# Four instead of three seven-product items in ten of twenty gate and up blocks, the norm's factor moved into the down product, and the mixer's constants moved to its own pool

## The chip, the cores and the metric

The kernel runs on one core of a Trainium2 chip, as one program. The metric is the time of one execution on the device in microseconds (us). The median of three runs of the kernel before is 2236.44 us (2235.84 to 2237.41). One more execution was profiled; its trace is what the figures of engines, lines and waits are read from.

TensorE (PE in the profile) multiplies; VectorE (DVE), ScalarE (ACT) and GpSimd (POOL) do element work; SyncE (SP) issues most transfers. Each engine works through its own list of instructions in order and waits on semaphores where an operand is not ready.

## What is computed

One decoder layer on `x` of 256 tokens by 2048 features, all float32:

```python
x = x + 0.5 * swiglu(rms_norm(x, ffn1_norm), ffn1_w_gate, ffn1_w_up, ffn1_w_down)
x = gated_parallel_mixer(x, ...)        # windowed attention beside an RWKV-7 recurrence
x = memory_cross_attention(x, mem, ...)
x = x + 0.5 * swiglu(rms_norm(x, ffn2_norm), ffn2_w_gate, ffn2_w_up, ffn2_w_down)
return rms_norm(x, final_norm)

def swiglu(h, w_gate, w_up, w_down):    # widths 2048 -> 5632 -> 2048
    return (jax.nn.silu(h @ w_gate) * (h @ w_up)) @ w_down
```

A norm's per-token factor `r` (called `rs` or `ms` in the trace) commutes with a product of matrices, so the kernel multiplies the un-normed `x` (with the gain on its features) by the weights and applies `r` to the result: `silu(r * gate)` and `r * up`.

## The kernel before

**Precision.** Each float32 weight tile is divided on chip into `hi` and `lo`, whose sum it is: ACT makes `hi` (L330), DVE makes `lo = raw - hi` (L331). `x` is divided likewise (`xhi`, `xlo`). One product of a 128x128 piece of `x` with a 128x512 piece of weights is three matmuls: hi by xhi, lo by xhi and hi by xlo (L422, L423, L424). Matmuls of the FFNs write 512 columns.

**Blocks and items.** Each of the two FFNs handles its 5632 columns in 11 blocks of 512, in groups of 4, 4 and 3 blocks, each group followed by its part of the down product. Block 0 is done with plain products; blocks 1 to 10 by `gate_up`, which calls `product_pair`. A block there is a row of eight items, q = 0 to 7. An item holds two of the 16 slices of 128 features (k-tiles) of the gate's and of the up's weights, four tiles of 128x512. A plain item takes eight products, 24 matmuls. An item of the other kind, a "seven", takes the seven products of a Strassen-like scheme on its 2x2 arrangement, 21 matmuls, on sums and differences of weight tiles and of pieces of `x`.

**What a seven needs.** `sums` forms the weights' differences on DVE: L350 (128x1024), L351 and L352 (128x512 each). ACT divides them into `thi` (L355, two of 128x1024), DVE into `tlo` (L356, two). There is one buffer of `thi` and one of `tlo`, so a seven's new `thi` can be written only when PE is done with that of the last seven. The tiles used as they are go through L330 and L331. The sums of `x` (`chi`, `clo`) are made once for each FFN by `combinations`, in the background of the first blocks; a chunk q whose item is a seven has four-term sums, and chunks 1 and 3, plain items between sevens, have a difference of two (`EARLY`). `SEVEN = (0, 2, 4)` says which items of a block are sevens; `SEVEN_DOWN = (2, 4)` does it for the down product's pairs.

**Order.** `next_item` hands out an item and divides the one ahead (`AHEAD`); `hi` and `lo` have three buffers, the weights' landing tiles (`raw2`) three. Background generators put work in between at each tick, and a scheduler orders the instructions of each engine by its own estimate of their times. The order is thus fixed when the kernel is built.

**End of a block.** `gate_up` adds the banks of PSUM: L559 to L561 after the last seven; at the block's end L567 and L570 on the gate's two halves, with SiLU on ACT behind each (L568, L571, `r` as its scale), and for the up's two halves L574 (add) and L575 (`scalar_tensor_tensor`, times `r` and times the gate), 128x512 each. In `down`, the factor 0.5 of the residual is applied in each `scalar_tensor_tensor` of `half` and, for pairs that are not done as sevens, at L778.

**Norms and constants.** `rs` of a norm is made from DVE's `ms` (L716) by POOL (L718). The masks and small matrices that the mixer needs (`identr`, `abias`, `mask3`, `bdmean`, `center`, `keep` and others, L213 to L244) are made by POOL at the kernel's start, in a pool that lives to its end, ahead of POOL's transfers of `attn_sinks`, `g_later` and `v_rwkv` (L247, L252). Copies of `x` to DRAM (`x1d`, L840) go out from POOL ahead of the mixer.

Of the kernel before, what the change touches and what calls it, by code (L numbers as in the profile page):

```python
# [15 lines left out]
P = 128  # L16
# [24 lines left out]
EARLY = tuple(q for q in range(max(SEVEN)) if q not in SEVEN)  # L41

SEVEN_DOWN = (2, 4)
# [46 lines left out]
def feed_forward_plan(wg, wu, wd):  # L90
    for gi, (j0, nj) in enumerate(GROUPS):
        for j in range(j0, j0 + nj):
            if j == 0:
                for w in (wg, wu):
                    yield w, 0, KD, j * 512, 512
            else:
                yield (wg, wu), 0, KD, (j * 512, j * 512), SEVEN
# [43 lines left out]
def decoder_layer(ctx: ExitStack, tc: tile.TileContext, a: dict, out: bass.AP):  # L141
# [71 lines left out]
    identr = cpool.tile([P, P], F32R, name="identr")  # L213
    select(identr[:], ones[:], [[-1, P]], ALU.is_equal, 0.0, 0, 1)
    abias = cpool.tile([P, 2, P], F32R, name="abias")
    pool.memset(f32(abias[:]), 0.0)
    select(abias[:, 0, :], abias[:, 0, :], [[1, P]], ALU.is_gt, NEG, 0, -1)
    select(abias[:, 1, :], abias[:, 1, :], [[-1, P]], ALU.is_ge, NEG, 0, 1)

    ups = cpool.tile([P, P], F32, name="ups")  # L220
    pool.memset(ups[:], UP)
    mask3 = cpool.tile([P, 3, P], F32, name="mask3")
    select(mask3[:, 0, :], ups[:], [[1, P]], ALU.is_gt, 0.0, 0, -1)
    select(mask3[:, 1, :], ups[:], [[1, P]], ALU.is_ge, 0.0, 0, -1)
    select(mask3[:, 2, :], ups[:], [[1, P]], ALU.is_ge, 0.0, 0, -1)

    mask_l = cpool.tile([P, P], F32, name="mask_l")
    select(mask_l[:], ups[:], [[-1, P]], ALU.is_gt, 0.0, 0, 1)
    bdones = cpool.tile([P, P], F32, name="bdones")
    bdmean = cpool.tile([P, P], F32, name="bdmean")  # L230
    bdup = cpool.tile([P, P], F32, name="bdup")
    pool.memset(bdones[:], 0.0)
    pool.memset(bdmean[:], 0.0)
    pool.memset(bdup[:], 0.0)
    for e in range(2):
        q = slice(64 * e, 64 * e + 64)
        pool.memset(bdones[q, q], 1.0)
        pool.memset(bdmean[q, q], 1.0 / 64)
        pool.memset(bdup[q, q], UP)
    center = cpool.tile([P, P], F32, name="center")  # L240
    dve.tensor_tensor(center[:], ident[:], bdmean[:], ALU.subtract)
    keep = cpool.tile([P, 2, P], F32, name="keep")
    pool.memset(keep[:], 1.0)
    pool.memset(keep[:, :, 0:1], 0.0)  # L244
# [23 lines left out]

    gneps = cpool.tile([P, 1], F32, name="gneps")
# [164 lines left out]
    def combinations(sp, x, seven, early, ready, tag, apart):  # L434


        n = 4 * len(seven) + 2 * len(early)
        parts = [sp.tile([P, n, P], F32R, tag=tag + e, name=tag + e) for e in ("hi", "lo")]
        c = {"parts": parts, "at": {}, "next": []}

        def work():
# [4 lines left out]
            for q in sorted(seven + early):  # L446
                while not all(KU * q + i in x.done for i in range(KU)):
                    yield
                v = sp.tile([P, 2, 2, P], F32, tag="u", name="u", bufs=2)
                f = sp.tile([P, 4, P], F32, tag="u", name="u", bufs=2)  # L450
                n = 4 if q in seven else 2
                s = slice(o, o + n)
                with behind_weights():
                    dve.tensor_tensor(
                        v[:].rearrange("p k t n -> p k (t n)"), f32(x.at(0, 2 * q, 2)),
                        f32(x.at(1, 2 * q, 2)), ALU.add,
                    )
                    if q in seven:
                        dve.tensor_tensor(f[:, 0], v[:, 0, 1], v[:, 1, 1], ALU.add)
                        dve.tensor_tensor(f[:, 1], f[:, 0], v[:, 0, 0], ALU.subtract)  # L460
                        dve.tensor_tensor(f[:, 2], v[:, 0, 0], v[:, 0, 1], ALU.subtract)
                        dve.tensor_tensor(f[:, 3], v[:, 1, 0], f[:, 1], ALU.subtract)
                    else:
                        dve.tensor_tensor(f[:, :2], v[:, :, 0], v[:, :, 1], ALU.subtract)
                yield from idle(2)
                with behind_weights():
                    act.copy(parts[0][:, s], f[:, :n])
                yield from idle(2)
                with behind_weights():
                    dve.tensor_tensor(  # L470
                        parts[1][:, s], f[:, :n], f32(parts[0][:, s]), ALU.subtract
                    )
                c["at"][q] = o
                o += n
                yield
# [4 lines left out]
    def product_pair(x: Act, c, w, four, seven, early, after, end, finish, first=()):  # L480
# [10 lines left out]
        def bank(to):  # L491
            if to in b:
                return
            for pair in PAIRS:
                if to in pair:
                    banks = two()
                    b.update((e, banks[:, i]) for i, e in enumerate(pair))
                    return
# [13 lines left out]
        def of_c(q, i):  # L512
            return [p[:, c["at"][q] + i, :] for p in c["parts"]]

        p5 = "p8" if four else "p5"
        for q in range(late + 1):
# [3 lines left out]
            if q in seven:  # L520
# [16 lines left out]
                continue  # L537
            u = next_item()
            for i in range(KU):
                for to, t, j in (("p2", 0, 0), ("p4", 1, 0), ("p3", 0, 1), (p5, 1, 1)):  # L540
                    off = to == "p3" and q in early
                    ends = last and i == KU - 1
                    add(to, of_c(q, i) if off else of_x(t, k + i), u[i][j], ends)
# [1193 lines left out]
```

## Time and profile before

| what | before |
| --- | --- |
| median of three runs | 2236.44 us (2235.84 to 2237.41) |
| the profiled execution, its time | 2236.75 us |
| its span in the trace | 2235.0 us |
| PE busy (matmuls) | 2216.0 us, 99% |
| DVE busy | 1745.4 us, 78% |
| ACT busy | 1193.5 us, 53% |
| POOL busy | 81.3 us, 4% |
| granted TensorE clock | 0.999 |

The span is the time between the first and the last instruction of the trace; the execution's time is 1.75 us longer, and that is 0.31 us above the median of the runs. A row of a timeline gives the start, the duration, the engine, the line of the code, the operation with its output and inputs, their shapes, and in brackets how long the engine was idle before it and what released it. Instructions of one engine overlap: the next one can begin before the last has ended, so the distance between two starts is what a row of instructions costs, not the sum of durations. Lines of the kernel before are L330 and so on; the same statements stand 15 to 25 lines further down in the changed one (L350 there is L365, L356 is L371, L331 is L346).

### The profile page before, as it was taken

To read this page: it belongs to the slowest core of one execution; us is meant where nothing else is said; L and a number is where in the kernel's file an instruction comes from. 1 tells how busy PE (TensorE), PEld (TensorE's weight loads), DVE (VectorE), ACT (ScalarE), POOL (GpSimd) and SP (SyncE) were. 2 spreads that over 40 slices of the span, in tenths; PEclk is the share of its full clock that TensorE was granted. 3 is DMA by queue.
4 is the path that set the end of the run, shared out by engine and by line. 5 is a ranking of instruction groups with operands and counts; after the bars stand their busy time and mean duration, and the time that the engine had idled before them with its cause. 6 is when DMAs were issued, how large, how long until landed. Compare 5 with 4: busy or idle time off the path is not lost.

```text
span 2235.0 us, 28341 instructions
## 1 busy us (share of the span) xinstructions
PE 2216.0 (99%) x10792; PEld 1819.2 (81%) x10792; DVE 1745.4 (78%) x2039; ACT 1193.5 (53%) x1434; POOL 81.3 (4%) x151
## 2 busy tenths in 40 slices
PE   9999999999999999999999999999999999999998
PEld 7888888888888877788888878888888888888886
DVE  7988988898987567886465466558888888898887
ACT  6555555555555567444443445556555555555554
POOL 1000000000000000103200100001000000000000
PEclk9999999999999999999999999999999999999999
DMA  7666665566556545677435775547665656566664
GB/s 247 211 220 195 203 207 190 187 208 202 194 193 214 165 130 151 219 219 233 121 102 148 230 266 189 181 164 255 201 207 177 218 193 199 193 202 194 207 203 155
DMA packets 219832, 435.40 MB, mean 195 GB/s; under 512 B 13888, under 2 KB 16016, under 8 KB 219696
## 3 DMA queue, kind: packets, MB, share of 16 engines
q1 hardware_dynamic: 210768, 406.37, 56.8%
q0 software_dynamic: 8352, 26.44, 3.8%
q8 instruction: 84, 1.38, 0.3%
q10 hardware_dynamic: 576, 0.79, 0.1%
q14 instruction: 52, 0.43, 0.1%
HBM read 420.05 MB, written 13.50 MB: 194 GB/s over the span
## 4 chain that ended last, share of the span: by engine, by line
PE 93%; DVE 3%; DMA 2%; ACT 1%; issue 1%; SPq 0%; POOLq 0%; POOL 0%; DVEq 0%; ACTq 0%
PE acc L422 20%; PE acc L423 20%; PE acc L424 20%; PE two L422 9%; PE two L423 9%; PE two L424 9%; PE two L185 2%; DVE lo L331 1%; PE two L177 1%; DMA raw<-in_ffn_w_up_dram 1%; DMA raw<-in_w_proj_rwkv_dram 1%; ACT hi L330 0%; PE two L1279 0%; DMA raw<-in_ffn_w_gate_dram 0%; PE acc L1416 0%
## 5 line engine op out<-in xcount | busy, mean ns | idle before, releaser
L330 ACT CAST hi<-raw 128x1024 fp32r<-128x1024 f32 (+1 forms) x770 | 764.2, 1001 | 783.7 <-PE acc L424 362.1
L331 DVE TENSOR_TENSOR lo<-raw,hi 128x1024 fp32r<-128x1024 f32 (+1 forms) x770 | 882.5, 1156 | 343.0 <-ACT hi L330 342.2
L422 PE MATMUL acc<-hi,xhi 128*128 128x512 f32 (+1 forms) x1256 | 491.2, 392 | 1.9 <-ACT hi L330 1.8
L423 PE MATMUL acc<-lo,xhi 128*128 128x512 f32 (+1 forms) x1256 | 488.2, 389 | 2.8 <-DVE lo L331 2.8
L424 PE MATMUL acc<-hi,xlo 128*128 128x512 f32 (+1 forms) x1256 | 486.9, 388 | 0.0
L422 PEld LDWEIGHTS acc<-hi,xhi 128*128 128x128 f32 x1256 | 235.7, 188 | 56.0 <-issue 5.4
L423 PEld LDWEIGHTS acc<-lo,xhi 128*128 128x128 f32 x1256 | 235.9, 188 | 55.2 <-DVE lo L331 6.7
L424 PEld LDWEIGHTS acc<-hi,xlo 128*128 128x128 f32 x1256 | 235.8, 188 | 47.4 <-DVE xlo L680 0.2
L356 DVE TENSOR_TENSOR tlo<-raw,thi 128x1024 fp32r<-128x1024 f32 x160 | 192.8, 1218 | 0.0
L355 ACT CAST thi<-raw 128x1024 fp32r<-128x1024 f32 x160 | 165.7, 1050 | 36.6 <-DVE raw L350 20.1
L423 PE MATMUL acc<-lo,hhi 128*128 128x512 f32 x424 | 166.4, 392 | 0.0
L424 PE MATMUL acc<-hi,hlo 128*128 128x512 f32 x424 | 165.2, 390 | 0.0
L422 PE MATMUL acc<-hi,hhi 128*128 128x512 f32 x424 | 159.8, 391 | 0.0
L422 PE MATMUL two<-hi,xhi 128*128 128x512 f32 x320 | 125.7, 393 | 0.0
L424 PE MATMUL two<-hi,xlo 128*128 128x512 f32 x320 | 124.6, 389 | 0.0
L423 PE MATMUL two<-lo,xhi 128*128 128x512 f32 x320 | 124.6, 389 | 0.0
L350 DVE TENSOR_TENSOR raw<-raw 128x1024 f32<-128x1024 f32 x80 | 97.5, 1219 | 15.4 <-DMA raw<-in_ffn_w_up_dram 13.1
L423 PEld LDWEIGHTS acc<-lo,hhi 128*128 128x128 f32 x424 | 79.6, 188 | 19.4 <-DVE lo L331 3.1
L422 PEld LDWEIGHTS acc<-hi,hhi 128*128 128x128 f32 x424 | 79.1, 188 | 18.6 <-ACT hi L330 2.6
L424 PEld LDWEIGHTS acc<-hi,hlo 128*128 128x128 f32 x424 | 79.6, 188 | 16.2
L422 PEld LDWEIGHTS two<-hi,xhi 128*128 128x128 f32 x320 | 60.1, 188 | 13.4 <-DVE u L574 0.2
L424 PEld LDWEIGHTS two<-hi,xlo 128*128 128x128 f32 x320 | 60.1, 188 | 12.6
(374 smaller groups left out, 3186.2 us busy)
## 6 DMA issues: line engine op xcount, KB each, us to landing
raw<-in_ffn_w_gate_dram SPq DMA_DIRECT2D x167, 512.0 KB, 3.8
raw<-in_ffn_w_up_dram SPq DMA_DIRECT2D x160, 512.0 KB, 4.7
raw<-in_ffn_w_down_dram SPq DMA_DIRECT2D x152, 512.0 KB, 4.8
raw<-in_w_in_dram SPq DMA_DIRECT2D x136, 512.0 KB, 3.7
raw<-in_w_out_dram SPq DMA_DIRECT2D x32, 512.0 KB, 3.6
raw<-in_ffn_w_down_dram SPq DMA_DIRECT2D x12, 1024.0 KB, 5.2
raw<-in_ffn_w_up_dram SPq DMA_DIRECT2D x8, 1024.0 KB, 7.9
raw<-in_w_proj_attn_dram SPq DMA_DIRECT2D x16, 512.0 KB, 4.2
```

Of the source, the lines that this page charges most:

```text
L177: prev = pe.matmul(to, lhs, rhs, **how)
L185: prev = pe.transpose(to, src, ident[:])
L330: newest["act"] = act.copy(hi[:, s], raw[:, s])
L331: newest["dve"] = dve.tensor_tensor(lo[:, s], raw[:, s], f32(hi[:, s]), ALU.subtract)
L350: dve.tensor_tensor(ta[:], raw[:, 1:3], raw[:, 0:2], ALU.subtract)
L355: act.copy(hi[:, s], t[:])
L356: dve.tensor_tensor(lo[:, s], t[:], f32(hi[:, s]), ALU.subtract)
L422: pe.matmul(o, xh, hi, start=first, stop=False, **how)
L423: pe.matmul(o, xh, lo, start=False, stop=False, **how)
L424: newest["pe"] = pe.matmul(o, xl, hi, start=False, stop=last, **how)
```

## The change

1. In blocks 3, 5, 7, 9 and 10 of both FFNs, item q = 3 becomes a seven as well (`MORE = (0, 2, 3, 4)`). Items 2, 3 and 4 are then three sevens in a row.
2. `combinations` makes both forms of the sums of `x` for chunk 3: the difference for blocks with three sevens, the four-term sums for those with four. Its temporaries move from the tag `u` (two buffers, shared with `gate_up`) to a tile `v` of their own with one buffer.
3. `gate_up` leaves `r` out of the up product. Its four 128x512 instructions at the end become two of 128x1024 over both halves (an add at L598, a product at L599), placed behind the last bank; PSUM's pair is now `("p3", "p5")`. `r` halved (`half`, two small multiplications for each FFN) replaces 0.5 where `down` adds to `x`: the factor of those `scalar_tensor_tensor` is read from a tile instead of being a constant, and the instructions in `down`'s `after` and `end` lose their 0.5.
4. The mixer's constants are made when the mixer's pool opens instead of at the kernel's start.

```diff
-EARLY = tuple(q for q in range(max(SEVEN)) if q not in SEVEN)
+MORE = (0, 2, 3, 4)
+def early(*sets):
+    return tuple(sorted({q for s in sets for q in range(max(s)) if q not in s}))
+def seven_up(j):
+    return MORE if j in (3, 5, 7, 9, 10) else SEVEN
...
-    identr = cpool.tile([P, P], F32R, name="identr")
+    def mixer_constants(sp):
+        identr = sp.tile([P, P], F32R, name="identr")
...
+    halves_ = cpool.tile([P, 4], F32, name="half")
...
-                v = sp.tile([P, 2, 2, P], F32, tag="u", name="u", bufs=2)
-                f = sp.tile([P, 4, P], F32, tag="u", name="u", bufs=2)
+                w = sp.tile([P, 2, 512], F32, tag="v", name="v", bufs=1)
+                todo = []
+                if q in seven:
+                    todo.append(4)
+                if q in minus:
+                    todo.append(2)
...
-    PAIRS = ("p6", "p7"), ("p5", "p3")
+    PAIRS = ("p6", "p7"), ("p3", "p5")
...
-            else:
-                t, v = (0, u2) if to == "p3" else (1, u3)
-                dve.tensor_tensor(v[:], b[to], v[:], ALU.add)
-                dve.scalar_tensor_tensor(
-                    hb[:, t], v[:], r[t], hb[:, t], ALU.mult, ALU.mult
-                )
+            elif to == "p5":
+                dve.tensor_tensor(u[:], b["p3", "p5"][:], u[:], ALU.add)
+                dve.tensor_tensor(hb[:], u[:], hb[:], ALU.mult)
...
-        def half(o, of, in1):
-            dve.scalar_tensor_tensor(o, of, 0.5, in1, ALU.mult, ALU.add)
+        def scaled_onto(t, o, v):
+            dve.scalar_tensor_tensor(o, v, r[t], o, ALU.mult, ALU.add)
...
-        c = combinations(sp, norm.x, SEVEN, EARLY, lambda: norm.r is not None, "c", 4)
+        c = combinations(
+            sp, norm.x, MORE, early(SEVEN, MORE), lambda: norm.r is not None, "c", 4
+        )
+        half = halves_[:, 2 * last : 2 * last + 2]
...
     with tc.tile_pool(name="mx", bufs=1, reuse_waits="tile") as sp:
         aligned(sp)
+        mixer_constants(sp)
```

In the built kernel PE has 10101 matmuls instead of 10131, all 30 fewer of the 128x512 form. DVE has 10 more of L350's kind, 20 more of L351's and L352's, and 20 more `tlo`; 10 fewer `lo` of 128x1024 and 10 more of 128x512; and 20 additions and 20 products of 128x1024 at the blocks' ends in place of 40 additions and 40 products of 128x512. SP's list has the same transfers; two loads of the mixer's weights stand two places from where they stood.

On DVE, here is the stretch around items 3 to 5 of block 3 in the first FFN, before (a number behind a name tells tiles of one name apart; L331 `lo`, L356 `tlo`, L350 to L352 the differences, `raw2` the landing tile):

```order
L350 TENSOR_TENSOR raw_1365<-raw2_1283 128x1024
L331 TENSOR_TENSOR lo_1333<-raw2_1246,hi_1332 128x1024
L331 TENSOR_TENSOR lo_1337<-raw2_1246,hi_1336 128x1024
L351 TENSOR_TENSOR raw_1366<-raw2_1283,raw_1365 128x512
L352 TENSOR_TENSOR raw_1366<-raw2_1283,raw_1366 128x512
L331 TENSOR_TENSOR lo_1377<-raw2_1283,hi_1376 128x1024
L356 TENSOR_TENSOR tlo_1368<-raw_1365,thi_1367 128x1024
L356 TENSOR_TENSOR tlo_1368<-raw_1366,thi_1367 128x1024
L331 TENSOR_TENSOR lo_1381<-raw2_1283,hi_1380 128x512
```

The same place on DVE in the changed kernel, from the first `tlo` of item 2 (tlo_1251) on; item 3's is tlo_1297, item 4's tlo_1341:

```order
L371 TENSOR_TENSOR tlo_1251<-raw_1248,thi_1250 128x1024
L367 TENSOR_TENSOR raw_1249<-raw2_1154,raw_1249 128x512
L346 TENSOR_TENSOR lo_1260<-raw2_1154,hi_1259 128x1024
L346 TENSOR_TENSOR lo_1264<-raw2_1154,hi_1263 128x512
L371 TENSOR_TENSOR tlo_1251<-raw_1249,thi_1250 128x1024
L365 TENSOR_TENSOR raw_1294<-raw2_1208 128x1024
L346 TENSOR_TENSOR lo_1306<-raw2_1208,hi_1305 128x1024
L366 TENSOR_TENSOR raw_1295<-raw2_1208,raw_1294 128x512
L346 TENSOR_TENSOR lo_1310<-raw2_1208,hi_1309 128x512
L367 TENSOR_TENSOR raw_1295<-raw2_1208,raw_1295 128x512
L365 TENSOR_TENSOR raw_1338<-raw2_1245 128x1024
L346 TENSOR_TENSOR lo_1350<-raw2_1245,hi_1349 128x1024
```

These rows make the third seven's differences beside the first one's `tlo`. On DVE the next rows follow directly and end with item 4's first `tlo`:

```order
L371 TENSOR_TENSOR tlo_1297<-raw_1294,thi_1296 128x1024
L371 TENSOR_TENSOR tlo_1297<-raw_1295,thi_1296 128x1024
L366 TENSOR_TENSOR raw_1339<-raw2_1245,raw_1338 128x512
L346 TENSOR_TENSOR lo_1354<-raw2_1245,hi_1353 128x512
L367 TENSOR_TENSOR raw_1339<-raw2_1245,raw_1339 128x512
L346 TENSOR_TENSOR lo_1382<-raw2_1291,hi_1381 128x1024
L371 TENSOR_TENSOR tlo_1341<-raw_1338,thi_1340 128x1024
```

Where two `lo` of a plain item stood between two sevens' work, a whole third seven stands. The order is the same in blocks 3, 5, 7 and 9 of both FFNs and a little different in block 10.

On PE, the item before the last seven of that block (item 3) before, a plain one whose last product is followed by item 4's first:

```order
L422 MATMUL two_1276<-hi_1336,xhi_151 128x512
L423 MATMUL two_1276<-lo_1337,xhi_151 128x512
L424 MATMUL two_1276<-hi_1336,xlo_152 128x512
L422 MATMUL acc_1257<-hi_1380,xhi_151 128x512
L423 MATMUL acc_1257<-lo_1381,xhi_151 128x512
L424 MATMUL acc_1257<-hi_1380,xlo_152 128x512
```

And on PE in the changed kernel, the end of item 3 and the start of item 4, up to the first matmul that reads item 4's `tlo`:

```order
L438 MATMUL two_1238<-lo_1350,chi_136 128x512
L439 MATMUL two_1238<-hi_1349,clo_137 128x512
L437 MATMUL acc_1223<-hi_1381,xhi_117 128x512
L437 MATMUL two_1227<-thi_1340,chi_136 128x512
L437 MATMUL two_1238<-thi_1340,chi_136 128x512
L438 MATMUL acc_1223<-lo_1382,xhi_117 128x512
L437 MATMUL acc_1234<-thi_1340,xhi_117 128x512
L439 MATMUL acc_1223<-hi_1381,xlo_118 128x512
L438 MATMUL two_1227<-tlo_1341,chi_136 128x512
```

The last row is the 58th matmul from the first of item 2. Some of item 4's products have moved ahead to where item 3's end.

On POOL, where the mixer begins, before (`x1d` is the copy of `x`, `rs` the norm's factor, `p` and `xu` padding):

```order
L718 TENSOR_TENSOR rs_355<-ms_353,nhalf_135 128x2
L840 DMA x1d_138<-x_149 128x2x512 x4
L1007 MEMSET p_6703 128x4
L1264 MEMSET xu_8605 32x1024
L718 TENSOR_TENSOR rs_5796<-ms_5793,nhalf_135 128x2
```

And on POOL there in the changed kernel, with the constants on both sides of `rs`:

```order
L861 DMA x1d_104<-x_115 128x2x512 x4
L212 AFFINE_SELECT identr_5776<-ones_72 128x128
L226 MEMSET abias_5778 128x256
L231 MEMSET ups_5786 128x128
L736 TENSOR_TENSOR rs_5769<-ms_5766,nhalf_101 128x2
L212 AFFINE_SELECT abias_5778<-abias_5778 128x128 x2
L212 AFFINE_SELECT mask3_5788<-ups_5786 128x128 x3
L212 AFFINE_SELECT mask_l_5792<-ups_5786 128x128
```

Three constants have come ahead of `rs`, and the rest stands behind it; on DVE the subtraction that makes `center` from them stands between two `lo` just behind `ms`.

185 lines of the change are left out of this document (99 added, 86 removed).

## The prediction, made before the changed kernel had run

> **What bounds the kernel now.** I read the page's first lines, then the time by stretches, then PE's waits, then timelines of a block with three sevens.
>
> ```profile
> span 2235.0 us, 28341 instructions
> PE 2216.0 (99%) x10792; PEld 1819.2 (81%) x10792; DVE 1745.4 (78%) x2039; ACT 1193.5 (53%) x1434; POOL 81.3 (4%) x151
> ...
> 300.00:400.00 100.00, 100.00 (x451) 82.92 (x450) 89.89 (x100) 57.19 (x63) 0.00 (x0) 1.00 0.61 200
> 1700.00:1800.00 100.00, 99.99 (x445) 82.25 (x443) 92.19 (x106) 52.96 (x57) 0.00 (x0) 1.00 0.62 200
> ...
> PE acc L423 <- DVE lo L331: 4.7, 8, 1.1
> PE two L185 <- DVE s L934: 1.8, 2, 0.9
> PE acc L422 <- ACT hi L330: 1.8, 2, 1.2
> ```
>
> PE is the bound: it is busy for 2216 of 2235 us, and its largest waits sum to 8.3 us. The columns of a stretch are its length, then busy time and count of PE, weight loads, DVE, ACT and POOL, the granted clock, the share of DMA and GB/s. In the FFNs, where the change lies, PE is full, at clock 1.00. But DVE has 8 to 10% left there, so PE's work can be cut only as far as DVE keeps up; the mean of 78% hides that. One matmul costs the distance between starts, from an item's first and last row and the next item's first:
>
> ```profile
> 362.85 0.39 PE L422 MATMUL acc<-hi,xhi 128*128 128x512 f32 x1
> ...
> 367.38 0.39 PE L424 MATMUL two<-thi,clo 128*128 128x512 f32 x1
> 367.61 0.39 PE L422 MATMUL acc<-hi,xhi 128*128 128x512 f32 x1
> ```
>
> 21 matmuls in 4.76 us are 0.2267 us each.
>
> **Part 1, the fourth seven: what it takes away.** Ten blocks lose 3 matmuls each: 30 x 0.2267 = 6.80 us, or 0.68 a block.
>
> **Part 1, what it adds on DVE.** These are rows of DVE and ACT in block 6 of the first FFN, whose item 2 is the one that starts on PE at 362.85; from item 2 backwards blocks 5, 7 and 9 are built like it.
>
> ```profile
> 351.45 0.68 DVE L567 TENSOR_TENSOR hb<-acc,hb 128x512 f32<-128x512 f32 x1
> 352.05 0.68 DVE L570 TENSOR_TENSOR hb<-acc,u 128x512 f32<-128x512 f32 x1
> 352.64 0.68 DVE L574 TENSOR_TENSOR u<-two,u 128x512 f32<-128x512 f32 x1
> 353.24 1.21 DVE L350 TENSOR_TENSOR raw<-raw 128x1024 f32<-128x1024 f32 x1
> 354.37 0.74 DVE L575 SCALAR_TENSOR_TENSOR hb<-u,rs,hb 128x512 f32<-128x512 f32 x1
> ...
> 357.43 1.22 DVE L331 TENSOR_TENSOR lo<-raw,hi 128x1024 fp32r<-128x1024 f32 x1
> 358.57 0.68 DVE L351 TENSOR_TENSOR raw<-raw,raw 128x512 f32<-128x512 f32 x1
> 359.17 1.22 DVE L356 TENSOR_TENSOR tlo<-raw,thi 128x1024 fp32r<-128x1024 f32 x1
> 360.31 0.68 DVE L352 TENSOR_TENSOR raw<-raw,raw 128x512 f32<-128x512 f32 x1
> 364.94 2.35 DVE L331 TENSOR_TENSOR lo<-raw,hi 128x1024 fp32r<-128x1024 f32 x2
> 369.67 2.35 DVE L356 TENSOR_TENSOR tlo<-raw,thi 128x1024 fp32r<-128x1024 f32 x2
> ...
> 352.16 0.73 ACT L568 ACTIVATE hb<-hb,rs 128x512 f32<-128x512 f32 x1 [1.36 <-DVE hb L567]
> 356.93 1.06 ACT L330 CAST hi<-raw 128x1024 fp32r<-128x1024 f32 x1 [1.44 <-PE two L424]
> 357.89 1.05 ACT L355 CAST thi<-raw 128x1024 fp32r<-128x1024 f32 x1
> ```
>
> A 128x1024 instruction is followed by the next start after 1.135 us (353.24 to 354.37, 357.43 to 358.57, 359.17 to 360.31 are 1.13 to 1.14), a 128x512 one after 0.60. A released engine starts some 0.03 after the releaser ends (L567 ends at 352.13, L568 starts at 352.16).
>
> In the changed order DVE goes from 351.45 through two 512s, L365, the merged add, a `lo`, the merged product, a `lo` and L366: 3 x 0.60 + 5 x 1.135 = 7.48, so it reaches item 2's first `tlo` at 358.93. Its `thi` ends on ACT at 358.94 (357.89 + 1.05), held by the cast at 356.93, which waits for PE. So `tlo` starts at 358.97. From there to item 4's first `tlo` are 10 instructions of 128x1024 and 8 of 128x512: 11.35 + 4.80 = 16.15 us if DVE is never idle. It starts at 375.12, ends 1.22 later at 376.34, and PE may go on at 376.37. PE wants it as the 58th matmul of the row: 362.85 + 57 x 0.2267 = 375.77. **The wait is 0.60 us.**
>
> What a wait costs beyond itself is seen where PE was held in block 3, by a late difference:
>
> ```profile
> 141.30 1.23 DVE L350 TENSOR_TENSOR raw<-raw 128x1024 f32<-128x1024 f32 x1 [0.31 <-DMA raw<-in_ffn_w_up_dram]
> ...
> 143.49 0.39 PE L424 MATMUL acc<-thi,xlo 128*128 128x512 f32 x1
> 143.84 0.50 PE L422 MATMUL two<-hi,chi 128*128 128x512 f32 x1
> 144.18 0.39 PE L423 MATMUL two<-lo,chi 128*128 128x512 f32 x1
> ```
>
> The held matmul takes 0.50 instead of 0.39 and its successor starts 0.34 later instead of 0.23: 0.11 on top. So eight blocks (3, 5, 7, 9, twice) lose 8 x 0.71 = 5.7 us. Against 0.68 saved, a block is back where it was.
>
> Block 10's list has 9 and 7 instructions there, so DVE is early; but there the single `thi` decides. PE last reads item 3's `thi` 42 matmuls behind item 2's first, in block 6's times at 372.37, until 372.76; ACT then needs 0.03 + 1.05, and PE, which wants item 4's `thi` 47 matmuls behind (373.50), goes on at 373.87 at best. That is 0.37 + 0.03 + 0.11 = 0.51, twice: 1.0 us. In the eight others `thi` is just in time: last read until 373.44, new one at 374.52, wanted at 374.64.
>
> A late load: in block 3 of the first FFN DVE already waits 0.31 for item 2's weights. The changed order asks for them 0.6 sooner (after two 512s instead of three), so DVE idles 0.9 there and PE pays that: +0.9. At 351.45 + 1.20 = 352.65 block 6 would need them; they land there at 352.1, and I take no loss in the others.
>
> **Part 2, the sums of x.** Chunk 3 gets four additions of 128x128, one copy and one `clo` more in each FFN, in the background of blocks 1 and 2:
>
> ```profile
> 55.00:70.00 15.00, 15.00 (x70) 12.15 (x70) 14.92 (x20) 9.18 (x10) 0.00 (x0) 1.00 0.56 177
> 85.00:100.00 15.00, 15.00 (x67) 12.30 (x67) 13.08 (x15) 9.37 (x11) 0.00 (x0) 1.00 0.64 219
> ...
> 69.88 0.28 DVE L459 TENSOR_TENSOR u<-u 128x128 f32<-128x128 f32 x1
> 70.08 0.28 DVE L461 TENSOR_TENSOR u<-u 128x128 f32<-128x128 f32 x1
> 72.95 0.68 DVE L470 TENSOR_TENSOR clo<-u,chi 128x512 fp32r<-128x512 f32 x1
> ```
>
> 4 x 0.20 + 0.60 = 1.4 us of DVE. Between 55 and 70 us DVE has 0.08 us free, between 85 and 100 it has 1.9. If all of it falls into the first stretch, PE loses up to 1.4; if into the second, nothing. I take 0.5 for each FFN: +1.0, bounds 0 and 2.8.
>
> **Part 3, r moved.** At a block's end four starts of 0.60 to 0.66 become two of 1.135: some 0.2 us of DVE less, already in the chain above; in blocks with three sevens DVE is a little earlier and PE does not wait there, so nothing. In `down` the factor read from a tile costs 0.06 more an instruction (0.74 for L575 against 0.68 for L574); these lie beside matmuls, except the last of the kernel:
>
> ```profile
> 2222.59 0.69 DVE L778 SCALAR_TENSOR_TENSOR x<-acc,x 128x512 f32<-128x512 f32 x1 [1.77 <-PE acc L424]
> 2226.66 0.69 DVE L778 SCALAR_TENSOR_TENSOR x<-acc,x 128x512 f32<-128x512 f32 x1 [0.30 <-PE acc L424]
> ```
>
> Two times 0.06: +0.1.
>
> **Part 4, the constants.** What stands ahead of `rs` on POOL, and who waits for it:
>
> ```profile
> 719.30 0.73 POOL L840 DMA_DIRECT2D x1d<-x  x1 [16.02 <-DVE x L778]
> 727.86 0.73 POOL L718 TENSOR_TENSOR rs<-ms,nhalf 128x2 f32<-128x2 f32 x1 [6.82 <-DVE ms L716]
> 739.55 0.69 ACT L990 ACTIVATE tok<-acc,rs 128x512 f32<-128x512 f32 x1 [0.35 <-PE acc L424]
> ...
> 731.07 1.22 DVE L331 TENSOR_TENSOR lo<-raw,hi 128x1024 fp32r<-128x1024 f32 x1 [1.50 <-ACT hi L330]
> ```
>
> POOL is idle for 6.82 us between `x1d` and `rs`; three constants ahead of it, and even several us of them, still leave `rs` ahead of its first reader 11 us later. `center` waits on DVE between two `lo`; the next `lo` has 1.50 us of idle ahead of it. I cost this at 0; if `center` has to wait for POOL beyond that cover, the `lo` behind it and then PE are late by the rest, bound 0 to 3 us. At the kernel's start POOL's three transfers go out some 4 us sooner, beside the first weights: 0, bound ±0.3.
>
> **Sum.** -6.8 + 5.7 + 1.0 + 0.9 + 1.0 + 0.1 = +1.9 us on the profiled execution's 2236.75. The median of the runs is 0.31 lower, so I say 2236.44 + 1.9 = 2238.3.
>
> **Against a rule.** The sum of DVE's chain goes by distances of starts. The Trainium skill's page "VectorE: DVE Perf Modes" says in its section "The DRAIN you can't avoid" that the next operation does not start until the pipe has emptied, and, in the same section, that one that is not held starts earlier. By the first half, 18 instructions would cost their durations, 10 x 1.22 + 8 x 0.68 = 17.64, and each block 1.49 more: some +15, 2253 us. The rows above disagree with it (two `lo` took 2.35, not 2.44; starts of 512s are 0.60 apart at a duration of 0.68) and go with the second half. I leave it a chance of 0.02, within the slower case.
>
> **The rivals.**
> 1. *DVE keeps up; faster.* Item 4's `tlo` comes in time because the chain starts sooner or is reordered by the waits in our favour. It needs 0.6 us in 16. For it: the chain's start hangs on ACT's cast behind PE, at 356.93, whose time the new order may move. Against it: DVE has no idle left in my chain, and the `thi` buffer holds item 4 at almost the same point (0.12 us of slack). Then the blocks cost only 0 to 0.1: -6.8 + 0.9 + 1.0 + 0.1 gives 2231.6; without the late load, 2230.7.
> 2. *DVE falls further behind; slower.* Place: the three sevens in each of the ten blocks. Four hand-overs there are within 0.1 us (`thi` of item 2 to `tlo`, item 3's first `tlo`, item 4's `thi`, and the load). If each block's loads or hand-overs are late as in block 3 (0.9 more), the sum is +1.9 + 8.1 (nine more blocks) = 2246.4. It decides from 0.27 us a block more: 10 x 0.27 + 1.9 = 4.6, over the 0.2% mark.
> 3. *The change doesn't do what it says* is excluded for the count: the built kernel has 30 fewer matmuls.
>
> **Chances and range.** 0.2% of 2236.4 is 4.5 us, which I take as about what a measurement tells from no change: 2232.0 to 2240.9. My forecast gets 0.52, own range 2234 to 2241; rival 1 gets 0.18; rival 2 gets 0.30, the rule's case included, since small mishaps in tight hand-overs add up on one side only. The range reaches to both rivals, 2231 to 2247.
>
> **What would show it.** In the profile after: item 3's and 4's matmuls with a wait of about 0.6 us on `tlo` (L438) once in each of blocks 3, 5, 7 and 9, and one on `thi` (L437) in block 10; DVE at 95% or more in these blocks; L365 waiting for a load some 0.9 in block 3; no new wait at L990 or on `rs`. I am wrong if PE's rows run through items 2 to 4 at 0.2267, or if waits stand at several places of one block, or if the time went into the mixer's start.

## The result, and the profile after

The changed kernel takes 2246.57 us (median of six runs, 2245.12 to 2248.80) against 2236.93 for the kernel before on the same chip (six runs): 9.6 us more, a ratio of 1.0043 (95% interval 1.0031 to 1.0055, clear of 1). The profiled execution took 2247.36 us. The time lies inside the stated range, at its upper end, and in the case "slower", which had a chance of 0.30; the likeliest case, 2238.3, did not come true.

The page of the changed kernel, with the columns of the page before:

```profile
span 2245.6 us, 28360 instructions
PE 2222.3 (99%) x10762; PEld 1807.7 (80%) x10762; DVE 1785.5 (80%) x2063; ACT 1203.4 (54%) x1456; POOL 80.1 (4%) x151
```

PE has 30 matmuls fewer and ends 10.6 us later. The start-to-start distances of its 128x512 matmuls show 17.4 us more above 0.227 each than before; less the 6.8 us saved that is the whole difference. What the distances of a stretch sum to above 0.227 for each matmul is called PE's excess below.

**Where it went, by stage.** An instruction that both kernels have can be used as a milestone: its start after less its start before is the loss up to there. Six pairs of rows, before first:

```profile
30.27 0.16 DVE L716 TENSOR_SCALAR ms<-acc 128x2 f32<-128x2 f32 x1 [0.92 <-PE acc L704]
96.64 0.68 DVE L567 TENSOR_TENSOR hb<-acc,hb 128x512 f32<-128x512 f32 x1
727.41 0.16 DVE L714 TENSOR_REDUCE ms<-ss 128x2 f32<-128x8 f32 x1
1289.38 1.28 DVE L1541 TENSOR_TENSOR gl<-acc,gl 128x512 f32<-128x512 f32 x2
1327.56 1.28 DVE L1541 TENSOR_TENSOR gl<-acc,gl 128x512 f32<-128x512 f32 x2
2158.98 0.69 DVE L567 TENSOR_TENSOR hb<-acc,hb 128x512 f32<-128x512 f32 x1 [1.09 <-PE acc L424]
```

```profile
31.85 0.16 DVE L734 TENSOR_SCALAR ms<-acc 128x2 f32<-128x2 f32 x1 [0.95 <-PE acc L722]
101.01 0.68 DVE L592 TENSOR_TENSOR hb<-acc,hb 128x512 f32<-128x512 f32 x1
736.10 0.16 DVE L732 TENSOR_REDUCE ms<-ss 128x2 f32<-128x8 f32 x1
1298.03 1.28 DVE L1569 TENSOR_TENSOR gl<-acc,gl 128x512 f32<-128x512 f32 x2
1333.89 1.28 DVE L1569 TENSOR_TENSOR gl<-acc,gl 128x512 f32<-128x512 f32 x2
2168.13 0.69 DVE L592 TENSOR_TENSOR hb<-acc,hb 128x512 f32<-128x512 f32 x1 [1.09 <-PE acc L439]
```

| stretch | offset at its end | its own loss |
| --- | --- | --- |
| start, to the first `ms` | +1.58 | 1.6 |
| first FFN to the end of block 1 | +4.37 | 2.8 |
| first FFN, the rest, to the mixer's `ms` | +8.69 | 4.3 |
| mixer, most of it | +8.65 | 0.0 |
| mixer, the product with `w_proj_rwkv` | +6.33 | -2.3 |
| rest of the mixer, cross-attention, second FFN to the end of block 10 | +9.15 | 2.8 |
| second FFN's last down product, end | +10.6 | 1.5 |

Two of these need care. The first is not the change's: PE ran at about half its clock for some 3 us, in the changed kernel's profiled execution and not in that of the kernel before (22 to 25 us, before, then after; the last three columns are the granted clock, the share of DMA and GB/s):

```profile
22.00:25.00 3.00, 3.00 (x15) 2.46 (x14) 3.00 (x6) 2.25 (x3) 0.00 (x0) 1.00 0.61 152
```

```profile
22.00:25.00 3.00, 3.00 (x9) 2.28 (x9) 3.00 (x6) 1.37 (x3) 0.00 (x0) 0.55 0.49 122
```

And in the product with `w_proj_rwkv` the kernel before had waited in its profiled execution, twice for about 0.8 us, with a loss of 1.0 us each by the distance of starts. Behind the first of them ACT had waited for a load of `w_proj_rwkv` itself:

```profile
1297.85 1.05 ACT L330 CAST hi<-raw 128x1024 fp32r<-128x1024 f32 x1 [3.76 <-DMA raw<-in_w_proj_rwkv_dram]
1300.21 0.50 PE L423 MATMUL acc<-lo,yr 128*128 128x512 f32 x1 [0.76 <-DVE lo L331]
1304.04 0.50 PE L423 MATMUL acc<-lo,yr 128*128 128x512 f32 x1 [0.77 <-DVE lo L331]
```

The profiles of the changed kernel and of all runs below lose 1.3 to 2.8 us less in this stretch. All of them have the mixer's constants moved, and the kernel before was profiled once, so it is not shown whether this loss was that execution's own or goes away with the constants.

What is left to the change are the two FFNs: 2.8 at the first one's head, the blocks, and each down product.

**The chain of a block with four sevens** came as worked out. Block 5 of the first FFN, on DVE, ACT and PE (the first row is the end of block 4):

```profile
314.53 0.68 DVE L592 TENSOR_TENSOR hb<-acc,hb 128x512 f32<-128x512 f32 x1
322.05 1.23 DVE L371 TENSOR_TENSOR tlo<-raw,thi 128x1024 fp32r<-128x1024 f32 x1
338.23 2.35 DVE L371 TENSOR_TENSOR tlo<-raw,thi 128x1024 fp32r<-128x1024 f32 x2
...
331.18 1.05 ACT L370 CAST thi<-raw 128x1024 fp32r<-128x1024 f32 x1
336.81 2.00 ACT L370 CAST thi<-raw 128x1024 fp32r<-128x1024 f32 x2 [2.17 <-PE acc L439]
...
332.28 0.50 PE L437 MATMUL two<-thi,chi 128*128 128x512 f32 x1
332.62 0.40 PE L438 MATMUL two<-lo,chi 128*128 128x512 f32 x1
...
338.49 0.39 PE L438 MATMUL acc<-lo,xhi 128*128 128x512 f32 x1
338.87 0.50 PE L437 MATMUL acc<-thi,xhi 128*128 128x512 f32 x1
339.20 0.40 PE L439 MATMUL acc<-hi,xlo 128*128 128x512 f32 x1
339.50 0.50 PE L438 MATMUL two<-tlo,chi 128*128 128x512 f32 x1
339.83 0.40 PE L439 MATMUL two<-thi,clo 128*128 128x512 f32 x1
```

From block 4's L592 to item 2's first `tlo` are 7.52 us (forecast 358.97 - 351.45 = 7.52), from there to item 4's first `tlo` 16.18 (forecast 16.15). PE gets to that `tlo` at 339.50 and not at 338.85. The delay is not one wait. PE breaks first on item 3's `thi`, at 332.28, just behind the cast that ends at 332.23, and has lost 0.17 there and at a `hi` 1.5 us later. Then it is held on the second half of item 4's `thi`, which ACT ends at 338.81, and two matmuls later on `tlo`; each of these breaks costs 0.11 on top. The same breaks stand in blocks 3 and 7, in block 9, and in these blocks of the second FFN.

In block 3 of the first FFN the load is late as forecast; DVE is idle for 0.94 us ahead of it:

```profile
145.66 1.22 DVE L365 TENSOR_TENSOR raw<-raw 128x1024 f32<-128x1024 f32 x1 [0.94 <-DMA raw<-in_ffn_w_up_dram]
```

### The profile page after: what moved, and what is told of

The parts are those of the page before. It is cut to its first block, busy times and chain, and to the rows that moved or that the text cites. A ratio compares the mean times of both kernels' runs of the same rounds, so it can differ in the third digit from the quotient of the medians.

```text
span 2245.6 us, 28360 instructions
## 1 busy us (share of the span) xinstructions
PE 2222.3 (99%) x10762; PEld 1807.7 (80%) x10762; DVE 1785.5 (80%) x2063; ACT 1203.4 (54%) x1456; POOL 80.1 (4%) x151
## 4 chain that ended last, share of the span: by engine, by line
PE 86%; DVE 8%; DMA 3%; issue 2%; ACT 1%; SPq 0%; POOL 0%; POOLq 0%; DVEq 0%; ACTq 0%
PE acc L438 19%; PE acc L437 19%; PE acc L439 19%; PE two L438 8%; PE two L437 8%; PE two L439 7%; DVE lo L346 3%; PE two L192 2%; DMA raw<-in_ffn_w_up_dram 1%; PE two L184 1%; DVE tlo L371 1%; DMA raw<-in_w_proj_rwkv_dram 1%; ACT hi L345 0%; DVE raw L365 0%; PE two L1307 0%
## 5 line engine op out<-in xcount | busy, mean ns | idle before, releaser
L437 PE MATMUL acc<-hi,xhi 128*128 128x512 f32 (+1 forms) x1236 | 482.4, 393 | 2.7 <-ACT hi L345 2.5
L439 PE MATMUL acc<-hi,xlo 128*128 128x512 f32 (+1 forms) x1236 | 480.2, 389 | 0.1
L370 ACT CAST thi<-raw 128x1024 fp32r<-128x1024 f32 x180 | 185.8, 1049 | 64.2 <-DVE raw L365 25.7
L371 DVE TENSOR_TENSOR tlo<-raw,thi 128x1024 fp32r<-128x1024 f32 x180 | 216.7, 1218 | 0.4 <-ACT thi L370 0.4
L365 DVE TENSOR_TENSOR raw<-raw 128x1024 f32<-128x1024 f32 x90 | 109.6, 1218 | 15.0 <-DMA raw<-in_ffn_w_up_dram 13.1
L437 PE MATMUL two<-hi,xhi 128*128 128x512 f32 x300 | 117.9, 393 | 0.0
L438 PE MATMUL two<-lo,xhi 128*128 128x512 f32 x300 | 116.8, 389 | 0.0
L439 PE MATMUL two<-hi,xlo 128*128 128x512 f32 x300 | 116.8, 389 | 0.0
L438 PE MATMUL two<-tlo,chi 128*128 128x512 f32 x210 | 82.9, 395 | 0.1
L437 PE MATMUL two<-thi,chi 128*128 128x512 f32 x210 | 82.2, 398 | 0.0
```

Source lines behind the costliest of these rows:

```text
L365: dve.tensor_tensor(ta[:], raw[:, 1:3], raw[:, 0:2], ALU.subtract)
L370: act.copy(hi[:, s], t[:])
L371: dve.tensor_tensor(lo[:, s], t[:], f32(hi[:, s]), ALU.subtract)
L437: pe.matmul(o, xh, hi, start=first, stop=False, **how)
L438: pe.matmul(o, xh, lo, start=False, stop=False, **how)
L439: newest["pe"] = pe.matmul(o, xl, hi, start=False, stop=last, **how)
```

## The experiments

All runs are compared with the kernel before on their own chip, whose median was 2236.65 (first four runs), 2236.62 (next four), 2236.28 (next three) and 2236.87 (last). Where runs of two groups are set against each other, it is by what each lies above or below its own; the changed kernel lies 9.6 us above. A step of 2 to 3 us between two runs is often within their intervals, so it is read together with the traces. L numbers are the changed kernel's.

**Three sevens again.**

```diff
 def seven_up(j):
-    return MORE if j in (3, 5, 7, 9, 10) else SEVEN
+    return SEVEN
```

> Three sevens in every block again; all else of the change stays, the second form of x's sums too (it is made and not used). Theory A, read from the two traces: the ten blocks with four sevens lose 9.7 us in waits and save 6.8 in matmuls, so they cost 2.9; this kernel is 2.9 us faster than the changed one, about 2243.7, still 6 to 7 us above the kernel before, because the rest of the loss lies at the first FFN's head (x's sums) and in the down products. Rival B: the sevens are the whole loss, since DVE behind them is late everywhere else too; then this kernel is at 2237.

Measured: 2243.03 us (ratio 1.0032, 1.0019 to 1.0044), 6.4 us above its kernel before and so 3.3 less than the changed kernel. The fourth sevens cost about 3 us net, as the 9.7 us of excess less 6.8 saved say, and are a third of the loss; rival B falls.

**And x's sums as before.**

```diff
-            sp, norm.x, MORE, early(SEVEN, MORE), lambda: norm.r is not None, "c", 4
+            sp, norm.x, SEVEN, early(SEVEN), lambda: norm.r is not None, "c", 4
```

> As the run before, and x's sums as in the kernel before: one form for each chunk. What is left is the factor moved into down, the merged ends of the blocks, the temporary of its own with one buffer, and the constants. Theory A: 2.3 to 2.8 us less than the run before (the head of the first FFN has lost that), about 2241; the 4 to 5 us above the kernel before that are left lie in down. Rival: the head's loss comes from the single buffer of the temporary and not from the second form; then this run is no faster than the one before it.

Measured: 2240.80 us (1.0018, 1.0009 to 1.0027), 2.2 less. The second form costs that; the end of block 1 comes 2.5 us earlier than in the run before. The single buffer of the temporary is not what hurts at the head.

**The factor back into the up product,** the rest of the change kept:

```diff
-            elif to == "p5":
-                dve.tensor_tensor(u[:], b["p3", "p5"][:], u[:], ALU.add)
-                dve.tensor_tensor(hb[:], u[:], hb[:], ALU.mult)
+            else:
+                t = 0 if to == "p3" else 1
+                dve.tensor_tensor(u[:, t], b[to], u[:, t], ALU.add)
+                dve.scalar_tensor_tensor(
+                    hb[:, t], u[:, t], r[t], hb[:, t], ALU.mult, ALU.mult
+                )
...
-            dve.scalar_tensor_tensor(o, v, r[t], o, ALU.mult, ALU.add)
+            dve.scalar_tensor_tensor(o, of, 0.5, in1, ALU.mult, ALU.add)
```

> Four sevens, both forms of x's sums and the constants stay; the factor goes back into the up product (four 128x512 instructions at a block's end, times r) and 0.5 into down. Theory A: down gets back its 4.7 us, the blocks lose up to 0.2 each because DVE has some 0.2 more to do in them, so 2242 to 2244. Rival C: down's loss is an accident of the order and has nothing to do with the factor; then it stays, and this run is at 2246.6 to 2248.6.

Measured: 2245.97 us (1.0040, 1.0026 to 1.0053), 0.3 less than the changed kernel. Theory A was wrong on this point: down's loss is not the factor's. In this run's trace nine of the ten blocks with four sevens have 1.02 to 1.08 us of excess on PE; in the changed kernel six of the ten have 0.82 to 0.87, the others 0.98 to 1.79. So the merged ends are worth some 0.2 in a usual block.

**All undone but constants and temporary** (the edit before this one, together with three sevens and x's sums in one form):

> Everything undone but the constants made in the mixer's pool and the temporary with one buffer. Theory A: the constants cost nothing, so 2236 to 2238, the kernel before. Rival D: constants and tiles are part of the loss; over 2239.

Measured: 2240.70 us (1.0016, 1.0007 to 1.0025). Theory A is wrong again, and the 4.0 us stand in a kernel without fourth sevens, second forms or moved factor. Its milestones against the kernel before put next to nothing (0.2) into the first 140 us, 0.4 to 0.5 into each of the first two down products of either FFN, and 1.3 to 1.4 into each last one (a loss of 1.5 in the mixer is another short stretch at half clock, and the gain of 1.6 in the `w_proj_rwkv` stretch makes it good). The constants lie elsewhere (the offset does not move around the mixer's start), so this pointed to the temporary in `combinations`, which down uses too. The order on DVE at each down product's start shows how: before, the second chunk's first sum goes ahead of the first chunk's last use, into the other buffer; after, with both in one tile, it has to stand behind it. Before (L454 the first sums, L470 `dlo`), then in the changed kernel (L473 and L492), at the last down product of the first FFN:

```profile
659.49 0.68 DVE L454 TENSOR_TENSOR u<-hhi,hlo 128x512 f32<-128x512 f32 x1
663.77 0.68 DVE L454 TENSOR_TENSOR u<-hhi,hlo 128x512 f32<-128x512 f32 x1
664.38 0.68 DVE L470 TENSOR_TENSOR dlo<-u,dhi 128x512 fp32r<-128x512 f32 x1
```

```profile
666.54 0.68 DVE L473 TENSOR_TENSOR v<-hhi,hlo 128x512 f32<-128x512 f32 x1
671.97 0.68 DVE L492 TENSOR_TENSOR dlo<-v,dhi 128x512 fp32r<-128x512 f32 x1
674.12 0.69 DVE L473 TENSOR_TENSOR v<-hhi,hlo 128x512 f32<-128x512 f32 x1
```

The two first sums are 4.28 us apart before and 7.58 after. The first seven's work and what follows are shifted in the engines' lists, and some 20 us later PE meets a `lo` that is late by 0.9 us:

```profile
692.51 0.45 PE L437 MATMUL two<-hi,hhi 128*128 128x512 f32 x1
693.86 0.50 PE L438 MATMUL two<-lo,hhi 128*128 128x512 f32 x1 [0.90 <-DVE lo L346]
694.20 0.40 PE L439 MATMUL two<-hi,hlo 128*128 128x512 f32 x1
```

By the distance of starts this wait costs 1.12 us here and 0.98 in the run just described; in the kernel before it is not there.

**Two tiles instead of one,** in the changed kernel; the space is the same:

```diff
-                w = sp.tile([P, 2, 512], F32, tag="v", name="v", bufs=1)
-                v = w[:, 0].rearrange("p (k t n) -> p k t n", k=2, t=2)
-                f = w[:, 1].rearrange("p (i n) -> p i n", i=4)
+                w = sp.tile([P, 512], F32, tag="v", name="v", bufs=1)
+                v = w[:].rearrange("p (k t n) -> p k t n", k=2, t=2)
+                f = sp.tile([P, 4, P], F32, tag="f", name="f", bufs=1)
```

> The changed kernel with one edit: x's sums' temporary is two tiles of one buffer each (first sum and the four sums apart) instead of one tile that holds both. Theory E: the single tile makes the second chunk's first sum wait for the last reader of the first chunk's sums, which moved the first seven's work of each down product and of the FFNs' first blocks; freed of that, the downs' 4.7 us and 1 to 2 us at the heads come back: 2240 to 2242. Rival D: the constants or the new offsets cost the time; then no change, 2246.6.

Measured: 2243.00 us (1.0031, 1.0019 to 1.0042), 3.3 less than the changed kernel. The downs' part of theory E holds: the two first sums are 4.28 us apart again, and the wait of 1.12 us above is 0.30 in this trace. The heads' part does not hold: with the clock's 1.6 taken off, 2.7 us are still lost there.

**The constants alone** (the kernel of the fourth experiment with the two tiles):

> The kernel before with the constants made in the mixer's pool and two temporaries of their own; no other part of the change. Theory E: the 4.0 us by which the run with the single tile stood above the kernel before are gone, 2236 to 2238. Rival D: they stay, 2240 to 2241.

Measured: 2235.58 us (0.9996, 0.9986 to 1.0005). This is the pair that shows the cause best: one tile or two, nothing else, 2240.70 against 2235.58 on two chips whose kernels before agree to 0.03, with their intervals apart (5.1 us). The wait in the last down product is gone from the trace. Constants in the mixer's pool cost nothing: `rs` is ready in time, and the mixer's first reader of it (`tok`) starts 12.14 us behind `ms` as before.

**The moved factor and the merged ends alone** (three sevens, one form, two tiles):

> Three sevens in every block and x's sums in one form, with two temporaries: what is left of the change is the factor moved into down and the merged ends of the blocks. Theory E: those two cost and bring nothing PE feels, 2236 to 2238. If moving the factor has a price of its own, it shows here alone.

Measured: 2237.14 us (1.0002, 0.9993 to 1.0011): no change. So the 9.6 us are, by medians against the kernel before on each chip, 3.3 for the fourth sevens, 2.2 for the second form, 3.6 for the single tile (the second run against this one) and 0.5 that cannot be told from nothing. These steps lead from one kernel to the other, so that they sum to 9.6 is no check on any of them.

**The merged product on GpSimd,** with two tiles:

```diff
-                dve.tensor_tensor(hb[:], u[:], hb[:], ALU.mult)
+                pool.tensor_tensor(hb[:], u[:], hb[:], ALU.mult)
```

> The changed kernel with two temporaries, and the merged product at a block's end (128x1024) on GpSimd instead of VectorE. Theory A, that the blocks' waits of 0.7 to 0.8 are DVE's 16 us of work between item 2's and item 4's tlo: the product is one of DVE's instructions ahead of that chain, not in it, and the chain's start hangs on ACT's cast; so only little comes back in blocks 3, 5, 7 and 9, 0 to 0.2 each, 2240 to 2242. Rival: DVE as a whole is too slow in these blocks and every instruction taken from it counts; 1.1 us a block are more than the wait, so the waits go and it is at 2234 or below. If GpSimd slows DVE down where both work, it is slower than the run with two temporaries.

Measured: 2285.85 us (1.0222, 1.0208 to 1.0236), 43 us slower than the run with two tiles. The last of the three outcomes came, and far stronger than thought. The product on POOL and what DVE did beside it:

```profile
150.10 3.25 POOL L599 TENSOR_TENSOR hb<-u,hb 128x1024 f32<-128x1024 f32 x1 [43.00 <-DVE u L598]
...
149.87 4.56 DVE L346 TENSOR_TENSOR lo<-raw,hi 128x1024 fp32r<-128x1024 f32 x2
151.01 3.43 DVE L346 TENSOR_TENSOR lo<-raw,hi 128x1024 fp32r<-128x1024 f32 x1
```

Two `lo` that take 2.35 us by themselves take 4.56 beside it. The last row is the second of them alone: 3.43 us instead of 1.22. DVE, relieved of 1.1 us, loses 2.2. The Trainium skill's page "SBUF — State Buffer" says in its section "SBUF: two separate sides" that the port pair which the two share is an exclusive lock, taken also by a VectorE instruction with two inputs in SBUF against a GpSimd one that reads SBUF; both instructions here are of that kind, and the trace goes with it: the first `lo`, under way when the product starts, takes its usual 1.22, and the second ends 1.09 us behind the product. So this run says nothing on whether DVE's time decides in the blocks.

**The fourth seven at item 6 instead of 3,** with two tiles:

```diff
-MORE = (0, 2, 3, 4)
+MORE = (0, 2, 4, 6)
```

> Two temporaries, and the fourth seven at item 6 instead of 3, so that no two sevens touch (x's sums then have four forms for chunks 0, 2, 4 and 6 and two for 1, 3 and 5). Compared with the two-temporaries run at 2243.0. Theory A (neighbours): the blocks' waits, 9.1 us in sum there, come from three sevens in a row on DVE; spaced, they fall to under 2 us in sum, less 0.5 to 1 for the one more difference at the heads: 2235 to 2238. Rival (capacity): DVE has only 1.7 us idle in blocks 5 and 9 with four sevens, whatever their places, and the block's end now meets a seven; waits stay at 0.7 to 1 a block, 2243 to 2245.

Measured: 2234.40 us (0.9991, 0.9982 to 0.9999), 8.3 less than the same kernel with neighbours, and just below the kernel before. Block 7 of the first FFN from its predecessor's L592 to its own, before, changed, spaced:

```profile
393.82 0.68 DVE L567 TENSOR_TENSOR hb<-acc,hb 128x512 f32<-128x512 f32 x1
435.62 0.69 DVE L567 TENSOR_TENSOR hb<-acc,hb 128x512 f32<-128x512 f32 x1 [1.09 <-PE acc L424]
```

```profile
399.41 0.68 DVE L592 TENSOR_TENSOR hb<-acc,hb 128x512 f32<-128x512 f32 x1
441.25 0.69 DVE L592 TENSOR_TENSOR hb<-acc,hb 128x512 f32<-128x512 f32 x1 [1.09 <-PE acc L439]
```

```profile
393.98 0.68 DVE L592 TENSOR_TENSOR hb<-acc,hb 128x512 f32<-128x512 f32 x1
435.17 0.68 DVE L592 TENSOR_TENSOR hb<-acc,hb 128x512 f32<-128x512 f32 x1
```

41.80, 41.84 and 41.19 us: with three sevens in a row the block gives back all that it saves, spaced it keeps 0.61 of 0.68. In the run with two tiles and neighbours this block takes 41.83. DVE has the same work in both (36.43 us busy in this block). Block 5, where DVE is fuller, says the same: DVE is busy for 41.19 of 42.88 us with neighbours and for 41.65 of 42.91 spaced, and PE's excess there is 0.84 and 0.18. From the end of block 3 to that of block 7, the three kernels take 254.51, 255.01 and 253.43 us, so spaced keeps 1.08 of the 1.36 saved in these two blocks. The rival, capacity, falls here: the waits come from the neighbourhood. Whether a second buffer of `thi` would take them away as well was not tried.

**The second form made later,** from block 2 on, with neighbours and two tiles; the core of the edit:

```diff
+        def extra_waits(q, n):
+            return apart > 0 and at["block"] < 2 and (n == 4 and q not in SEVEN or q > max(SEVEN))
...
-            for q in sorted(set(seven + minus)):
+            for q, n in jobs:
+                while extra_waits(q, n):
+                    yield
```

> Two temporaries, sevens at 0, 2, 3 and 4 as in the change, but the second form of x's sums of chunk 3 is made only from block 2 on (it is needed in block 3), at the price of one more first sum. Theory: the 2.2 to 2.8 us at the first FFN's head are DVE's lack of time in block 1; in block 2 DVE has 4.8 us idle and takes them: 2240 to 2241. Rival: an extra sum costs wherever it lies, since the order of DVE there is broken up by it; 2243.

Measured: 2240.63 us (1.0018, 1.0009 to 1.0027), 2.0 less than the run with two tiles. The head shows it: by the end of block 2, with the clock aside, this run has lost 0.3 us against the kernel before, the changed kernel 2.8. As expected: the second form costs where it lies, in a block in which DVE has no time.

**Both.**

> Both edits: sevens at 0, 2, 4 and 6, and the forms that only these need made from block 2 on. If both theories hold, the 6.8 us of matmuls come through less some 2 us: 2231 to 2234, below the kernel before. If the spaced sevens only move the waits, 2240 or more.

Measured: 2235.55 us (0.9993, 0.9984 to 1.0002), no better than the spaced run alone. Between the expected cases: by the end of block 2 the spaced order had lost only 0.9 us against the kernel before, where neighbours had lost 2.8 (the clock aside), and this run 1.1, so nothing was won there. Why the same work costs less at the head of the spaced order was not settled.

**Spaced, in blocks 3 to 10,** with two tiles:

```diff
 MORE = (0, 2, 4, 6)
...
-    return MORE if j in (3, 5, 7, 9, 10) else SEVEN
+    return MORE if j >= 3 else SEVEN
```

> Two temporaries, sevens at 0, 2, 4 and 6 in blocks 3 to 10 of both FFNs, so in six blocks more than in the spaced run at 2234.4 (blocks 4, 6 and 8). Theory (neighbours only): each of the six saves 0.68 less some 0.2 of waits: 2231 to 2232. Rival (capacity): in block 6 DVE had 3.9 us idle with three sevens and a fourth adds 3.9, in block 5 it has 1.3 left with four; with several such blocks in a row DVE has nothing left and falls behind by its surplus: waits of 0.5 to 1.5 in each of these blocks, 2234 to 2240.

Measured: 2231.66 us (0.9977, 0.9968 to 0.9986), 5.2 us below the kernel before on its chip: faster than both kernels, and as the neighbours theory had it; a few blocks still wait (block 6 of the first FFN has 1.10 us of excess). DVE is then all but full (300 to 400 us; the busy times are those of PE, weight loads, DVE, ACT, POOL):

```profile
300.00:400.00 100.00, 99.59 (x445) 81.42 (x444) 97.78 (x105) 59.89 (x67) 0.00 (x0) 1.00 0.61 200
```

## Why the prediction was right or wrong, point by point

- *The matmuls taken away* and *PE as the bound*: right. 30 fewer, and the saved time is there as soon as the sevens are spaced.
- *The chain on DVE in blocks 3, 5, 7 and 9*: right in size, and the chain itself to 0.03 us; not right in being one wait on `tlo`. The prediction's own sign of being wrong, waits at several places of one block, came: PE is held on `thi` of items 3 and 4 as well. The working had item 4's `thi` in time by its first half alone; the second half follows 0.95 us behind it and is wanted three matmuls, 0.68 us, later, so by the same rows it is late. PE's excess over the kernel before in these eight blocks is 1.49 (block 3, first FFN), 0.80, 0.72, 0.83, and 0.72, 1.01, 0.72, 0.78 us, forecast 0.71, and 1.61 for the first with its late load. DVE is busy for 96% of blocks 5 and 9, as forecast, and for 85 to 87% of blocks 3 and 7, which end a group.
- *Block 10*: too small. 1.74 and 0.88 us instead of 0.51 each. In the run with two tiles the first block has an excess of 1.10, but also 1.02 in the run with the factor back, which has the single tile; what the rest hung on is open. The ten blocks lost 9.7 us instead of 7.6; against 6.8 saved that is 2.9, forecast 0.8, and the experiment says 3.3.
- *The sums of x*: mis-sized. The term of 1.0 us for both FFNs measured 2.0 to 2.2 by the experiments, nearly all of it in the first, above the 1.4 that was its bound for one FFN. The working counted DVE's extra microseconds and not that a DVE without slack makes PE wait at several places, with a restart each.
- *Not costed at all*: the single tile of the temporary, 3.3 to 5.1 us. The step that failed is the one that treated part 2 as four additions, a copy and a `clo`: the same part also changed which instructions may pass each other, in all six down products as well, and that was not worked out though the order of instructions in the changed kernel, known when it was built, shows it. It is as large as the sevens.
- *The moved factor and the constants*: right, nothing that can be told from no change, together (with 0.5 us) and for the constants alone. The factor alone has no run; the two runs that differ by it and the merged ends are 1.6 us apart, within their intervals.
- *The rivals*: the time fell where rival 2 had it, 2246.4, but not by its mechanism. The blocks are not each late by 0.9 more; the down products and the first FFN's head are late instead. That 2246.4 was met is luck: a sum that lands near the number is no proof of its terms. The forecast itself, 2238.3, was 8.3 us too low; its range held the result only because it reached to this rival.
- *The rule against*: the 18 instructions took 16.18 us, where the sum of their durations, which is what the first half of the Trainium skill's page "VectorE: DVE Perf Modes" in "The DRAIN you can't avoid" would make of them, is 17.64. The trace disagrees with it and goes with the second half.
- *The sum's base*: the profiled execution before held a loss of 2.3 us in the mixer that none of the other profiles has, whatever its cause, and the profiled execution after a stretch at half clock that cost 1.6. They pull in opposite directions, and the difference of medians, 9.6, is not far from the traces' 10.6.

## What to carry to other kernels

When temporaries are put together into one tile, work out which of its parts live longest: a shared buffer makes the next round's first write wait for this round's last read, and an order planned around that moves work that has nothing to do with it. Extra work on an engine with 90% load is cheap or dear by where it lies: three heavy items in a row cost PE 0.7 to 0.8 us in most blocks (up to 1.7), the same work with a light item between them 0.3 or less. And before adding up one profiled execution, look for losses in it that other executions of the same kernel do not have, on both sides of the comparison.

## What the runs showed of the hardware that was not expected

- GpSimd and VectorE on tiles of 128x1024 float32 at the same time slowed each other down: 4.56 us instead of 2.35 for two VectorE instructions beside a GpSimd product of 3.25 us, and 43 us over 20 such products. They took turns: the VectorE instruction already under way ended as usual, the product ended 2.26 us behind it, whether it had started 0.99 ahead of that end (3.25 us long) or 0.51 ahead (2.77 us long), and the next VectorE instruction ended 1.09 us behind the product.
- The granted TensorE clock fell to half for 3.41 us near 22 us, in some executions and not in others, and cost 1.6 us. The changed kernel's runs with a mean clock of 0.999 took 2245.1 to 2245.8 us, those with 0.998 or 0.997 took 2247.4 to 2248.8. The clock changes in steps of 3.41 us. In the step just ahead of the fall, in which PE had waited for weights, PE was busy for 1.57 us; in the kernel before, whose steps lie elsewhere, the same gap is shared by two steps, with 2.23 us in the emptier one, and the clock stays. The step ahead of the fall and the fall itself, then the two steps of the kernel before (counted back from the fall at the end of its trace):

```profile
17.90:21.31 3.41, 1.57 (x6) 0.67 (x4) 3.31 (x3) 3.41 (x5) 0.00 (x0) 1.00 1.05 409
21.31:24.72 3.41, 3.21 (x8) 2.53 (x9) 3.41 (x7) 2.06 (x4) 0.00 (x0) 0.50 0.57 163
```

```profile
17.02:20.43 3.41, 2.23 (x10) 1.33 (x8) 3.41 (x7) 3.10 (x4) 0.00 (x0) 1.00 1.03 384
20.43:23.85 3.42, 2.58 (x12) 1.99 (x11) 3.42 (x6) 2.87 (x6) 0.00 (x0) 1.00 0.75 244
```

  The four other profiles with a fall there (two tiles, two tiles with three sevens, the product on GpSimd, spaced and late) have 1.35 to 1.64 us in the step ahead of it. The Trainium skill's page "TensorE: Matmul & The Clock Gate" ("Part 1: The HAM clock gate") has a gate at half rate that judges PE's activity in windows of 3.4 us which run on their own, so that the same gap may or may not count; the steps here and the 0.43 us from start to start agree with it. Busy time is not all that counts: in three runs the clock also fell in the mixer, near 1126 to 1130 us, behind a step in which PE was busy throughout with 103 to 109 matmuls, most of them smaller. No run tried to move the fall.
